# RMSNorm and QKV projection: DMA transposes from tile 6, stores in three parts, three staging buffers for wide weight chunks

## The chip, the cores and the metric

One core of one Trainium2 chip. The metric is the device time of one execution in microseconds (us). Engines: PE is the TensorE, PEld its weight loads, DVE the VectorE, ACT the ScalarE, POOL the GpSimd. SP is the SyncE, whose sequencer (SPq) issues nearly every DMA of this kernel, in program order.

## The reference

```python
def reference(x, gamma, w_qkv, eps):       # x: 8 x 1024 x 768, w_qkv: 768 x 2304, float32
    rms = np.sqrt(np.mean(x ** 2, axis=-1, keepdims=True) + eps)
    x_norm = x / rms * gamma
    return np.matmul(x_norm, w_qkv).astype(np.float32)
```

8192 rows make 64 tiles of 128 rows. A tile needs 6 blocks of K times 2304 columns of matmul, in bf16.

## The kernel before

x comes in as float32, is cast to bf16 and transposed, because the matmul needs K on the partitions. gamma goes into the weights, 1/rms into the evacuation of PSUM (the copy of a matmul's result out of the buffer in which the TensorE leaves it). The first six tiles (the head) are worked through while the six weight chunks arrive, chunk by chunk; the other 58 run tile by tile. Each operation is given a planned time, and all are issued in the order of those times.

```python
ARRIVALS = "wxxxwxxwxwww"                   # order of the head's loads
C0 = [0, 256, 2048, 512, 1024, 1536]        # columns at which the weight chunks begin
CHUNKS = [256, 256, 256, 512, 512, 512]
FIRST_XBAR = 12                             # first tile that a DMA transposes
...
PARTS = [(0, 1024), (1024, N - 1024)]       # a row of the output is stored in two parts
...
def load_w(c):
    n = CHUNKS[c]
    WF[c] = wst.tile([P, KO, n], f32, name=f"w_f{n}", bufs=3 if n == 256 else 2)
    nc.sync.dma_start(out=WF[c], in_=wv[:, :, C0[c]:C0[c] + n])
...
def trans_pe(t):                            # 6 transposing matmuls into PSUM, then copy_xT on DVE
    PT[t] = psum_t.tile([P, KO, P], bf16, name="pt")
    for ko in range(KO):
        nc.tensor.transpose(out=PT[t][:, ko, :], in_=XB[t][:, ko * P:(ko + 1) * P], identity=ident)
def trans_dma(t):
    XT[t] = xTp.tile([P, KO, P], bf16, name="xT")
    nc.sync.dma_start_transpose(out=XT[t], in_=XB[t])
...
for t in range(HEAD, MT):                   # HEAD is 6, MT is 64
    T = state["pe"]                         # planned start of the tile on PE
    at(T - 15, load_x, t)
    if t < FIRST_XBAR:
        at(T - 4.5, cast_x, t)
        at(T - 3.0, trans_pe, t)
        at(T - 2.5, copy_xT, t)
    else:
        at(T - 8.5, cast_x, t)
        at(T - 7.5, trans_dma, t)
    at(T - 5, stat, t)
    at(T - 3, recip, t)
    for n0, nl in n_tiles:                  # 4 blocks of 512 columns and one of 256
        unit(t, n0, nl)                     # matmuls, evacuation; store of a part when it is full
```

## Time and profile before

| | before |
|---|---|
| median of its runs | 394.45 us (393.62 to 394.56, 4 runs) |
| span of the profiled run | 392.1 us |
| PE busy | 98%, and 97% of the chain that ended last |
| transposing matmuls | 72, in 12 tiles |
| DMA packets' time, as a share of 16 engines' span | 97.1% |

The span is from the first to the last instruction; the time is some 2 us more. The chain that ended last is followed back from the last instruction, at each step to what released it. The lines that carry the argument (busy shares, the chain in order of time, three stretches) are shown and read in the prediction.

### The profile page before, as it was taken

The page shows a single profiled execution, that of the slowest core. Times are in us where ns is not written, and L with a number is a line of the kernel's source. Part 1 is how long each engine was busy: PE and PEld are TensorE (multiplying, and loading weights), DVE is VectorE, ACT ScalarE, POOL GpSimd, SP SyncE. Part 2 cuts the span into 40 slices and gives each one's busy share as a digit, 9 for nine tenths or more (in the row PEclk, how much of TensorE's full clock was granted, in tenths as well). Part 3 has the DMA queues.
Part 4 walks back from the last instruction along what each step waited for, and adds up shares of the span by engine and source line. Part 5 has one row for each costly group of instructions (what it writes and reads, how often), then busy time and mean ns, then how long its engine had stood idle before and what let it go on. Part 6 is the DMA issues. An engine that isn't in the chain of part 4 may idle for free.

```text
span 392.1 us, 5550 instructions
## 1 busy us (share of the span) xinstructions
PE 383.7 (98%) x2037; PEld 197.0 (50%) x2037; DVE 158.1 (40%) x319; ACT 182.8 (47%) x369; POOL 8.0 (2%) x18
## 2 busy tenths in 40 slices
PE   5999999999999999999999999999999999999996
PEld 2764455555455445545545545545545545545543
DVE  3853434443333433343434333434333443333332
ACT  5664344354444354345344445444444445444432
POOL 1221000000000000000000000000000000000000
PEclk9899999999999999999999999999999999999999
DMA  8989696899999999999999999999999999999974
GB/s 273 381 283 405 241 396 257 289 274 303 318 299 296 286 327 292 326 291 285 342 288 311 309 263 339 310 295 312 298 304 295 308 315 298 298 317 293 303 260 192
DMA packets 74423, 118.34 MB, mean 302 GB/s; under 512 B 44822, under 2 KB 47260, under 8 KB 74396
## 3 DMA queue, kind: packets, MB, share of 16 engines
q1 hardware_dynamic: 74384, 117.98, 97.1%
q8 instruction: 16, 0.26, 0.3%
q14 instruction: 11, 0.09, 0.1%
q10 hardware_dynamic: 12, 0.00, 0.0%
HBM read 32.25 MB, written 75.50 MB: 275 GB/s over the span
## 4 chain that ended last, share of the span: by engine, by line
PE 97%; DMA 1%; DVE 0%; ACT 0%; SPq 0%; issue 0%
PE pm L133 95%; DMA x_t<-in_x_dram 1%; PE pt L120 1%; DVE xb L102 0%; ACT ot L148 0%; DVE xT L124 0%; SPq L88 0%; ACT w_b L96 0%
## 5 line engine op out<-in xcount | busy, mean ns | idle before, releaser
L133 PE MATMUL pm<-w_b,xT 128*128 128x512 bf16 (+1 forms) x1956 | 376.4, 355 | 0.1
L133 PEld LDWEIGHTS <-xT 128*128 128x128 bf16 x1956 | 191.2, 98 | 181.4 <-issue 0.3
L146 DVE TENSOR_SCALAR ot<-pm,rstd 128x512 f32<-128x512 f32 (+1 forms) x163 | 112.2, 689 | 215.0 <-PE pm L133 200.5
L148 ACT ACTIVATE ot<-pm,rstd 128x512 f32<-128x512 f32 (+1 forms) x163 | 103.8, 637 | 199.6 <-PE pm L133 138.9
L107 ACT ACTIVATE sq<-x_t 128x768 bf16<-128x768 f32 x64 | 53.3, 832 | 0.0
L102 DVE CAST xb<-x_t 128x768 bf16<-128x768 f32 x64 | 35.1, 548 | 0.1
L109 ACT ACTIVATE rms<-ssq,eps_sb 128x1 f32<-128x1 f32 x64 | 18.9, 295 | 2.1
L107 ACT ACTIVATION_READ_ACCUMULATOR sq<-x_t 128x1 f32 x64 | 12.2, 191 | 0.0
L124 DVE COPY xT<-pt 128x768 bf16<-128x768 bf16 x12 | 6.7, 557 | 10.6 <-PE pt L120 10.3
L120 PE MATMUL pt<-ident,xb 128*128 128x128 bf16 x72 | 6.7, 235 | 3.6 <-DVE xb L102 3.5
L114 DVE RECIPROCAL rstd<-rms 128x1 f32<-128x1 f32 x64 | 9.8, 153 | 0.0
L96 ACT ACTIVATE w_b<-w_f,g_sb 128x256 bf16<-128x256 f32 (+1 forms) x12 | 6.7, 605 | 3.3 <-DMA w_f<-in_w_qkv_dram 3.3
L120 PEld LDWEIGHTS <-xb 128*128 128x128 bf16 x72 | 5.1, 104 | 6.1 <-DVE xb L102 4.7
L98 POOL TENSOR_SCALAR w_b<-w_f,g_sb 128x256 bf16<-128x256 f32 (+1 forms) x12 | 7.3, 623 | 23.9 <-DMA w_f<-in_w_qkv_dram 23.9
L94 DVE TENSOR_SCALAR w_b<-w_f,g_sb 128x256 bf16<-128x256 f32 (+1 forms) x12 | 4.9, 453 | 0.6 <-DMA w_f<-in_w_qkv_dram 0.6
L169 PE MATMUL pm<-warm 128*128 128x512 bf16 x8 | 3.6, 630 | 1.2 <-DVE warm L67 1.2
L169 PEld LDWEIGHTS <-warm 128*128 128x128 bf16 x8 | 1.0, 140 | 2.9 <-issue 1.7
L70 ACT ACT_TABLE_LOAD x1 | 1.3, 1283 | 1.3 <-PEq L247 1.3
L164 DVE COPY g_sb<-pt 128x6 f32<-128x6 f32 x1 | 0.2, 165 | 3.5 <-PE pt L163 3.5
L163 PEld LDWEIGHTS pt<-ident_f,g 6*128 6x128 f32 x1 | 0.2, 178 | 0.8 <-issue 0.8
L65 DVE MEMSET eps_sb<- 128x1 f32 x1 | 0.1, 59 | 0.8 <-PEq L247 0.8
L74 DVE CAST ident<-ident_f 128x128 bf16<-128x128 f32 x1 | 0.2, 226 | 0.2 <-POOL ident_f masks.py:199 0.2
(9 smaller groups left out, 1.6 us busy)
## 6 DMA issues: line engine op xcount, KB each, us to landing
out_dram<-ot SPq DMA_DIRECT2D x63, 640.0 KB, 3.9
out_dram<-ot SPq DMA_DIRECT2D x63, 512.0 KB, 3.9
x_t<-in_x_dram SPq DMA_DIRECT2D x64, 384.0 KB, 4.6
w_f<-in_w_qkv_dram SPq DMA_DIRECT2D x3, 1536.0 KB, 13.0
w_f<-in_w_qkv_dram SPq DMA_DIRECT2D x3, 768.0 KB, 6.4
out_dram<-ot SPq DMA_DIRECT2D x4, 256.0 KB, 2.0
xT<-xb SPq DMA_TRANSPOSE x52, 4.2
out_dram<-ot SPq DMA_DIRECT2D x1, 128.0 KB, 2.0
```

The lines of the kernel that those rows point to most:

```text
L94: nc.vector.tensor_scalar(out=o, in0=i, scalar1=g, scalar2=None, op0=mult)
L96: nc.scalar.activation(out=o, in_=i, func=AF.Copy, scale=g, bias=0.0)
L98: nc.gpsimd.tensor_scalar(out=o, in0=i, scalar1=g, scalar2=1.0, op0=mult, op1=mult)
L102: nc.vector.tensor_copy(out=XB[t], in_=X[t])
L107: nc.scalar.activation(out=sq, in_=X[t], func=AF.Square, accum_out=ssq)
L109: nc.scalar.activation(out=rms, in_=ssq, func=AF.Sqrt, scale=inv_k, bias=eps_sb)
L114: nc.vector.reciprocal(out=r, in_=RS[t])
L120: nc.tensor.transpose(out=PT[t][:, ko, :], in_=XB[t][:, ko * P:(ko + 1) * P], identity=ident)
L124: nc.vector.tensor_copy(out=XT[t], in_=PT[t])
L133: nc.tensor.matmul(out=PM[t, n0][:, :nl], lhsT=XT[t][:, ko, :], rhs=w_b[:, ko, n0:n0 + nl], start=(ko == 0), stop=(ko == KO - 1))
L146: nc.vector.tensor_scalar(out=o, in0=pm[:, :nl], scalar1=RS[t], scalar2=None, op0=mult)
L148: nc.scalar.activation(out=o, in_=pm[:, :nl], func=AF.Copy, scale=RS[t], bias=0.0)
```

## The change

Three edits. DMA transposes take tiles 6 to 11 off PE. Rows leave in three parts of 4096, 4096 and 1024 bytes. And all three wide weight chunks have a buffer at once, so that no load waits for one.

```diff
-FIRST_XBAR = 12
+FIRST_XBAR = 6
...
-    PARTS = [(0, 1024), (1024, N - 1024)]
+    PARTS = [(0, 1024), (1024, 1024), (2048, N - 2048)]
...
-        WF[c] = wst.tile([P, KO, n], f32, name=f"w_f{n}", bufs=3 if n == 256 else 2)
+        WF[c] = wst.tile([P, KO, n], f32, name=f"w_f{n}", bufs=3)
```

## The prediction

> **What bounds the kernel now.** I read the page first (busy shares, slices), then the chain that ended last in order of time, then stretches of the span, then the waits of the DMA queue. The busy shares name the TensorE, and the chain settles it, because a busy PE alone would not:
>
> ```profile
> PE 383.7 (98%) x2037; PEld 197.0 (50%) x2037; DVE 158.1 (40%) x319; ACT 182.8 (47%) x369; POOL 8.0 (2%) x18
> PE 97%; DMA 1%; DVE 0%; ACT 0%; SPq 0%; issue 0%
> L120 PE MATMUL pt<-ident,xb 128*128 128x128 bf16 x72 | 6.7, 235 | 3.6 <-DVE xb L102 3.5
> ```
>
> The chain is PE for 97% of the span, and nearly all of it is the main matmul (L133). L120 is the transposition of x on the PE: 12 tiles of 6. The chain in order of time shows what one such tile costs (start, length, what; all in us):
>
> ```profile
> 20.26 25.30 PE pm L133 x138
> 45.57 0.34 PE pt L120 x6
> 45.90 6.47 PE pm L133 x30
> 52.38 0.34 PE pt L120 x6
> 52.71 5.83 PE pm L133 x30
> 58.55 0.34 PE pt L120 x6
> ...
> 64.72 0.34 PE pt L120 x6
> 65.05 5.83 PE pm L133 x30
> 70.89 0.34 PE pt L120 x6
> 71.22 5.83 PE pm L133 x30
> 77.06 0.34 PE pt L120 x6
> 77.39 311.22 PE pm L133 x1602
> ```
>
> Three things are to be seen. From 20.26 on the PE waits for nothing. The six pieces of 0.34 between 45.57 and 77.06 are tiles 6 to 11, which come 6.17 apart, 5.83 of main matmuls and 0.34 of transposition. From 77.39 on, where DMA transposes feed the tiles, one piece of main matmuls runs to 388.61. (The 6.47 is no loss: the plan puts the transposes 3 us ahead of a tile, and the thirty matmuls between those two are five blocks of 512 columns, at 1.295 each, instead of four and a half.)
>
> The second resource is the DMA. Columns: length of the stretch; busy time and count of PE, PEld, DVE, ACT, POOL; PE clock; DMA share; GB/s.
>
> ```profile
> 52.00:60.00 8.00, 8.00 (x50) 4.29 (x49) 3.55 (x7) 3.18 (x6) 0.00 (x0) 1.00 1.02 389
> 60.00:77.00 17.00, 17.00 (x99) 8.99 (x98) 8.09 (x16) 7.73 (x16) 0.00 (x0) 1.00 0.71 253
> 100.00:340.00 240.00, 240.00 (x1235) 120.66 (x1234) 93.42 (x185) 111.77 (x226) 0.00 (x0) 1.00 1.03 304
> ```
>
> PE is full in each. The DMA share is 0.71 where the PE transposes and 1.03 where the DMA does, and yet the PE keeps 5.83 a tile. A share over 1 comes of packets that overlap, so 1.03 is not proof of a bound, only of little room.
>
> **What the Trainium skill says.** "TensorE: Matmul & The Clock Gate", section "Wait — 56ns, not 53.3ns?": warm matmuls follow each other at N/2.4 GHz plus about 2.5 ns, 55.6 ns for N = 128 and 215.7 for 512. The trace agrees: 24 x 215.7 + 6 x 109.2 (N = 256) = 5.83 us a tile, and 6 x 55.6 = 0.33 against the 0.34 in the chain. So the PE is at its issue rate, and the listed mean of 235 ns for a transposing matmul is latency, not cost. The same page, "Part 4: PE-mode transpose", gives about 275 ns in one kernel's context; that would make six cost 1.65, and the chain's 0.34 decides against using it as a cost here. "Advanced Engine Details and Errata", section "X-Bar Transpose (TRN2)", calls transposing DMAs as fast as ordinary ones. The trace differs: in 60:77 a tile takes 0.71 x 6.17 = 4.4 us of the DMA engines for 1.57 MB (0.39 in, 1.18 out), later 1.03 x 5.83 = 6.0; the 0.2 MB of a transpose thus add 1.6 us, where 0.55 would be in proportion (estimates, as packets overlap). "DMA: Bandwidth & Descriptors", section "Rules for kernel authors", advises coalescing small transfers; the third store part goes against it, and is priced below.
>
> **The change, part by part.**
>
> *DMA transposes from tile 6.* Removed from the PE: 6 tiles x 6 = 36 matmuls, all on the chain: 6 x 0.34 = 2.04 us. Removed from DVE: 6 copies from PSUM, 6 x 0.56 = 3.4 us, beside a PE that does not wait for DVE. Added: 6 DMA transposes, about 1.6 us of DMA each, in a stretch (45 to 77) that partly has room (0.71), and 6 issues on the DMA queue of about 1.6 us each. On the path: nothing, if they land in time. In the steady part the transpose for tile 12 was issued at 76.95, landed at 81.01, and the tile began at 85.2: 4 us of slack. For tile 6 there is less. It begins near 48.2 (48.5 before, less its own 0.34). The cast is planned 8.5 earlier, at 39.7, and x of tile 6 landed at 38.7 in the kernel before, so the issue is near 40.7. Stores in that stretch took 5.6 to 6.2 us to land against a median of 3.9, so I take 6: landed at 46.7, 1.5 us in hand. Tile 7: issue near 46, landing near 52, start near 54. Tile 8: issue near 52.3, landing near 58.3, start near 59.8.
>
> *Three store parts.* A row of 9216 bytes went as 4096 + 5120 and will go as 4096 + 4096 + 1024. In the trace's packet records the medians are 201 ns for 5120 bytes, 159 for 4096, 46 for 1024. So a tile has 8 packets more for each DMA engine and 8 x (159 + 46 - 201) = 32 ns more of its time, some 0.5% of 5.83. On the queue: one more issue a tile at 0.33, to 1.6 + 0.4 + 3 x 0.33 = 3.0 us of the 5.83. Part two leaves one block of 256 columns (0.65) earlier. In the head, six stores of the 256-column chunk can leave near 25 us instead of after 42, which makes the burst at 42 to 58 smaller (512 KB each instead of 640). In the tail nothing changes: the last tile is stored block by block in both.
>
> *Staging for all wide chunks.* The queue's longest wait goes:
>
> ```profile
> SPq L88 <- DVE w_b L94: 12.9, 1, 12.9
> ```
>
> The load of the last wide chunk was issued at 24.34 and landed at 31.06; it will be queued right behind the chunk that landed at 25.52 and arrive about 1 us sooner. Worth on the path: 0, because the chain has no wait from 20.26 on.
>
> Sum: -2.04 + 0 + 0. PE ends near 386.6, and the fixed end after it (392.1 - 388.6 = 3.5) stays: span 390.1. Time: 394.36 - 2.04 = 392.3.
>
> **The rivals.**
>
> *The early transposes come late.* The burst of head stores and its 1.02 share speak for it, the 1.5 us in hand, the smaller burst, and the six banks of PSUM (6.5 us of matmuls that need no evacuation) against it. If tiles 6, 7 and 8 each miss by 0.7 to 1, the gain is gone: 394.4, hardly over 395.
>
> *The DMA becomes the bound.* A share of 1.03 speaks for it. Against it: at the median packet times a tile needs 8 x (121 for a row of x, 3072 bytes, + 159 + 201) + 48 x 18 ns (256-byte transpose packets) = 4.7 us of each engine, 81% of 5.83, and the change adds 0.03. If I am wrong and the small packets cost 0.1 us on each of 52 tiles, 397.
>
> *The early chunk gains.* It would if the PE waited for weights; the chain shows no such wait after 20.26, and the earlier ones are for chunks whose issue does not change. If it did: 391.
>
> **Range and chances.** I take the first account, 392.3. The time before varies by 0.9 between its runs (393.62 to 394.54), which sets the width more than the mechanisms do; I stretch it upward for the first rival: 391.3 to 393.6. Over 2% faster would need under 386.5, with 5.8 us more than the change removes from the path: 0.01. Over 2% slower would need over 402.2, 0.19 us a tile lost from tile 6 on: 0.02. Within 2%: 0.97.
>
> **What would show it right or wrong.** Right: L120 falls to 36 matmuls; the last PE transposition in the chain is of tile 5, near 20; from there one piece of L133 to about 386.6 with tiles 5.83 apart; DMA share between 60 and 77 up from 0.71 to about 1. The queue has no wait of 12.9 on the last chunk, and the chunk lands near 30. Wrong: a wait of PE or its weight load on a DMA transpose between 45 and 62 (first rival); gaps that recur in the steady part, landings that grow beyond 4.2 (second); a different chain before 20.

## The result, and the profile after

| | before | after |
|---|---|---|
| median | 394.45 us | 392.41 us (392.06 to 392.93, 4 runs) |
| ratio | | 0.9954, 95% interval 0.9936 to 0.9972 |
| span of the profiled run | 392.1 us | 390.4 us |

A ratio is the mean time of one kernel's fast runs over that of the other's of the same rounds, so not quite the ratio of the medians. 392.3 had been predicted. The lines of the page that answer to those of before:

```profile
PE 380.2 (97%) x1964; PEld 195.6 (50%) x2001; DVE 154.4 (40%) x313; ACT 182.9 (47%) x369; POOL 8.1 (2%) x18
L133 PE MATMUL pm<-w_b,xT 128*128 128x512 bf16 (+1 forms) x1919 | 373.8, 355 | 2.1 <-ACT w_b L96 0.2
L120 PE MATMUL pt<-ident,xb 128*128 128x128 bf16 x36 | 4.0, 265 | 3.2 <-DVE xb L102 3.2
```

The transposing matmuls are halved, 72 to 36. One trap: L133 has 1919 matmuls here and 1956 before. Nothing was left out of the program; 37 records are missing from this trace (the weight loads are all 1956). Each missing one shows as a gap of some 0.05 us, which makes up most of the 2.1 us of idle time and cuts the chain, here in order of time (start, length, what), into many pieces:

```profile
16.80 3.27 PE pm L133 x30
20.41 5.88 PE pm L133 x48
26.34 10.74 PE pm L133 x49
37.13 10.74 PE pm L133 x49
...
379.65 7.10 PE pm L133 x38
386.77 0.47 ACT ot L148
```

No L120 piece stands between 20.41 and the end, where six stood before, and PE's last piece ends at 386.75, with 386.6 predicted. The stretches of the kernel after, with the columns as in the prediction:

```profile
52.00:60.00 8.00, 7.95 (x43) 4.19 (x43) 3.15 (x6) 3.18 (x6) 0.00 (x0) 1.00 1.06 361
60.00:77.00 17.00, 16.95 (x87) 8.42 (x87) 6.67 (x14) 7.88 (x17) 0.00 (x0) 1.00 1.05 341
100.00:340.00 240.00, 238.74 (x1214) 121.04 (x1237) 93.15 (x185) 112.36 (x226) 0.00 (x0) 1.00 1.03 305
```

From 60 to 77 the DMA share is 1.05 instead of 0.71: the transposes have moved there. The steady share of 1.03 is as before, three parts or two.

**A measure without the noise.** The times of one kernel differ by up to 1.7 us, which is near the size of the effect. The traces show where that comes from: the 151st main weight load, in the middle of the head, starts anywhere between 33.2 and 34.4 us in the fourteen traces. (In the two profiles of the changed kernel the spans differ by 0.74 us, and this start by 0.75.) From there to the last weight load, kernels that run the same PE program without a wait agree to 0.01 us. I call this the PE stretch. It is 354.68 before and 352.67 after: 2.01 us less, the 36 transposing matmuls at 56 ns.

### The profile page after: what moved, and what is told of

It reads as the page before. It is cut to its first block, busy times and chain, and to the rows that moved or that the text cites. A ratio compares the mean times of both kernels' runs of the same rounds, so it can differ in the third digit from the quotient of the medians.

```text
span 390.4 us, 5527 instructions
## 1 busy us (share of the span) xinstructions
PE 380.2 (97%) x1964; PEld 195.6 (50%) x2001; DVE 154.4 (40%) x313; ACT 182.9 (47%) x369; POOL 8.1 (2%) x18
## 4 chain that ended last, share of the span: by engine, by line
PE 96%; DMA 1%; issue 1%; DVE 0%; ACT 0%; SPq 0%
PE pm L133 95%; DMA x_t<-in_x_dram 1%; PE pt L120 1%; DVE xb L102 0%; ACT ot L148 0%; DVE xT L124 0%; SPq L88 0%; ACT w_b L96 0%
## 5 line engine op out<-in xcount | busy, mean ns | idle before, releaser
L133 PE MATMUL pm<-w_b,xT 128*128 128x512 bf16 (+1 forms) x1919 | 373.8, 355 | 2.1 <-ACT w_b L96 0.2
L133 PEld LDWEIGHTS <-xT 128*128 128x128 bf16 x1956 | 191.8, 98 | 182.9 <-issue 0.4
L120 PE MATMUL pt<-ident,xb 128*128 128x128 bf16 x36 | 4.0, 265 | 3.2 <-DVE xb L102 3.2
L120 PEld LDWEIGHTS <-xb 128*128 128x128 bf16 x36 | 2.8, 117 | 4.3 <-DVE xb L102 4.1
L124 DVE COPY xT<-pt 128x768 bf16<-128x768 bf16 x6 | 3.3, 556 | 2.6 <-PE pt L120 2.4
```

The source lines that it names most:

```text
L133: nc.tensor.matmul(out=PM[t, n0][:, :nl], lhsT=XT[t][:, ko, :], rhs=w_b[:, ko, n0:n0 + nl], start=(ko == 0), stop=(ko == KO - 1))
```

## The experiments

Each kernel gave a correct result.

### One part alone, and the change without its first part

`e1_transposes_only`: the kernel before, with `FIRST_XBAR = 6`.

> The kernel before with DMA transposes from tile 6 on, and nothing else of the change. Theory (the gain is 36 PE transposes off a PE-bound path, 0.34 us a tile): 392.3, 2.0 us below the kernel before, with 36 instead of 72 transposing matmuls. Rival (the stores and the staging make the room that the early transposes need, or bring part of the gain): clearly above 392.3, 393.5 or more, with a PE wait near tiles 6 to 9.

`e2_transposes_undone`: the changed kernel, with `FIRST_XBAR = 12`.

> The changed kernel with the first DMA transpose back at tile 12; three store parts and staging stay. Theory: the kernel before within 0.5 us, 394.4; the last chunk of weights still lands near 30 us, and that is worth nothing. Rival (staging or stores bring the gain): near 392.4.

`e5_parts_only`: the kernel before, with the three `PARTS`.

> The kernel before with three store parts alone. Theory: 394.4, within 0.5 us of the kernel before, although 63 more stores are issued and packets are smaller. Rival (the DMA is at its limit at a share of 1.03, so 32 ns a tile or more goes into the tile's period): 396 or more. Second rival (the parts help and hide a loss from staging): under 393.6.

`e6_staging_only`: the kernel before, with `bufs=3` for all chunks.

> The kernel before with a third buffer for wide weight chunks alone. Theory: the 12.9 us wait of the DMA queue goes, the last chunk lands about 1 us sooner, and the time stays 394.4 within 0.5 us. Rival (the head waits for weights in a way the chain hides): 393.6 or less.

Five rounds each, on one chip; the kernel before had a median of 394.15 there.

| kernel | median, us | ratio to before (95%) | PE stretch, us |
|---|---|---|---|
| transposes only | 393.37 | 0.9986 (0.9973 to 0.9999) | 353.56 |
| transposes undone (parts and staging) | 394.25 | 1.0006 (0.9990 to 1.0022) | 354.68 |
| parts only | 393.83 | 0.9998 (0.9981 to 1.0014) | 354.68 |
| staging only | 394.33 | 1.0004 (0.9990 to 1.0018) | 354.68 |

Parts and staging are worth nothing alone or together: the PE stretch is that of the kernel before to the hundredth. But the first run went against the theory. The transposes alone should have given 2.0 us and gave 0.8; the stretch shortens by 1.12 instead of 2.01. Its trace shows where 0.89 us went. Of the waits, those of the PE for a DMA (total, times, longest):

```profile
PEld L133 <- DMA xT<-xb: 1.0, 1, 1.0
PE pm L133 <- DMA xT<-xb: 0.7, 1, 0.7
```

One wait, seen twice: the weight load, and the matmul behind it, waited once for a transpose. (Tile 8's weight load was 0.12 us late too, too little for this list.) The chain of the same kernel between 58 and 69 us, in part, shows which:

```profile
58.60 1.36 PE pm L133 x8
59.96 6.82 DMA xT<-xb
66.78 0.05 issue
66.82 2.12 PE pm L133 x9
```

The fourth DMA transpose, that of tile 9, was issued at 59.96 and took 6.82 us to land (until the last of its parts was reported done), against a median of 4.2 for those whose landing the trace tells. Tile 9 could start only at 66.82. This is the first rival of the prediction (the early transposes come late), and here it is true, once. In the changed kernel the same transpose was issued at 58.20 and landed at 63.44, 2.1 us before its tile. So the lead is short there too, and something else in the change protects it. That became the new question.

### The size of the PE cost, and the room of the DMA

`e3_pe_until_36`: the changed kernel, with `FIRST_XBAR = 36`.

> The changed kernel with PE transposes up to tile 35: 30 tiles more than the changed kernel has. Theory (0.34 us of PE time a tile, no more and no less): 392.4 + 30 x 0.34 = 402.6. Rival (the DMA at a share of 1.03 sets a good part of the tile's period, so relieving it pays back): well under 402.6, 400 or less. Second rival (a PE transpose costs the 235 to 275 ns that a single one shows): 30 x 6 x 0.235 = 42 us more, 435.

Measured: 402.57 us (3 rounds), ratio 1.0201 (1.0184 to 1.0218). The PE stretch is 362.72, 10.05 more than in the changed kernel: 30 tiles x 0.335. The chain of this kernel, and two stretches of it, one with PE transposes and one with DMA transposes:

```profile
102.19 0.34 PE pt L120 x6
102.53 5.83 PE pm L133 x30
108.36 0.34 PE pt L120 x6
108.70 5.83 PE pm L133 x30
```

```profile
100.00:180.00 80.00, 80.00 (x469) 42.43 (x467) 36.13 (x72) 35.37 (x72) 0.00 (x0) 1.00 0.71 256
260.00:340.00 80.00, 80.00 (x414) 40.34 (x413) 30.53 (x60) 37.50 (x76) 0.00 (x0) 1.00 1.05 305
```

The DMA share falls from 1.05 to 0.71 where the PE transposes, and buys nothing: a tile's main matmuls take 5.83 in both. That settles that the DMA, with its share over 1, does not set the steady pace.

`e4_five_parts`: the changed kernel, with `PARTS` of 512, 512, 512, 512 and 256 columns.

> The changed kernel with rows stored in five parts, 4 of 2048 bytes and one of 1024. By the packet medians (85 ns for 2048 bytes against 159 for 4096) this adds 8 x (4 x 85 - 2 x 159) = 176 ns of each DMA engine's time a tile, and two issues of 0.33 us on the queue. Theory (4.7 of 5.83 us needed, hence room): 392.4 within 0.5. Rival (the DMA is the bound, or shares it): 58 x 0.18 = 10 us more, 402.

Measured: 392.53 us (3 rounds), ratio to the kernel before 0.9944 (0.9924 to 0.9964); the PE stretch is 352.67, as in the changed kernel. 126 more stores (tiles 0 to 62, two more each) with rows of 2048 bytes cost nothing. The transpose of tile 9 landed 3.9 us before its tile here; that of tile 6 had 1.5 us in hand, where it has 4.2 in the changed kernel. So this run only shifts which tile is tight, and none is late.

### How much lead a transpose needs

`e7_transposes_3us_later` and `e8_transposes_5us_later`: the changed kernel, with

```diff
-            at(T - 8.5, cast_x, t)
-            at(T - 7.5, trans_dma, t)
+            at(T - 5.5, cast_x, t)             # e8: T - 3.5
+            at(T - 4.5, trans_dma, t)          # e8: T - 2.5
```

> The changed kernel with cast and DMA transpose planned 3 us later (4.5 instead of 7.5 ahead of the tile). Theory (the transposes are hidden by about 4 us of lead, landing takes 4.3): the lead is nearly used up, issue near 5 us ahead: 392.4 to 395, with short PE waits in the crowded stretch of tiles 8 to 10 only. Rival (the lead does not matter, throughput does): 392.4 and no waits. Second rival (the lead was already short): above 400.

> As the last, with cast and transpose 5 us later than in the changed kernel (2.5 ahead). Theory: the transpose is issued about 2.7 us into the tile before and takes 4.3 to land, so a tile cannot start less than about 7.0 us after the one before: 58 x (7.0 - 5.83) = 68 us more, about 460, and the PE waits at each tile on the transpose. Rival (only throughput counts): 392.4.

| kernel | median, us | ratio to before (95%) | PE stretch, us | median issue, ahead of the tile |
|---|---|---|---|---|
| changed | 392.41 | 0.9954 (0.9936 to 0.9972) | 352.67 | 7.4 us |
| 3 us later | 395.77 | 1.0036 (1.0015 to 1.0057) | 355.93 | 4.9 us |
| 5 us later | 414.85 | 1.0514 (1.0493 to 1.0535) | 375.32 | 3.7 us |

3 us later lands a little above the expectation, and not where it said. The median lead left at landing is 0.4 us, so most tiles just make it, but four waits of note stand at 53.7, 165.8, 265.8 and 365.7; only the first is in the crowded stretch. The other three each begin 1 to 2 us after a packet of 16,384 bytes of the program's own instructions (at 164.2, 264.6 and 363.6), which takes a DMA engine for 0.9 to 1.2 us. Over the traces this is no accident. Take the transposes from tile 14 on whose landing can be told, in all traces but that of the next run: 125 had such a packet between issue and landing, with a median of 4.7 us, and 21 of them took over 5.4 us; 405 had none, with a median of 4.2, and the longest took 5.37. No run moved the packets, so the statistics show a link, not yet a cause.

5 us later, the work is unchanged and the time is 22 us longer: the transposes are on the path. In its list of waits:

```profile
PEld L133 <- DMA xT<-xb: 26.2, 32, 2.0
PE pm L133 <- DMA xT<-xb: 17.2, 25, 1.8
```

The kind of wait was as expected; its size and its number were not: 22.65 us more PE stretch, 0.39 a tile, where 68 us had been expected. Every tile was to lose 1.17; 32 of 58 waited, 0.8 us each. I had put the issue 3.1 us ahead of the tile and the landing at 4.3 us. Measured: 3.7 ahead in the median (to the tile's start as it was, waits included), and 3.7 to land. The DMA was emptier too (a share of 0.92 from 100 to 340 us, against 1.03); that this shortened the landings was not tested.

### What protects the early transposes

`e9_transposes_and_staging`, `e10_transposes_and_parts`: the changed kernel with one of the two other parts undone. `e11_transposes_only_2us_earlier`: the kernel before with

```diff
-FIRST_XBAR = 12
+FIRST_XBAR = 6
-        at(T - 15, load_x, t)
+        at(T - 17, load_x, t)
-            at(T - 8.5, cast_x, t)
-            at(T - 7.5, trans_dma, t)
+            at(T - 10.5, cast_x, t)
+            at(T - 9.5, trans_dma, t)
```

and `e12_changed_again`: the changed kernel.

> DMA transposes from tile 6 and staging, rows in two parts. New theory after the run with the transposes alone (393.4, with one PE wait of 0.84 us on the transpose of tile 9, which came 6.8 us after its issue in the crowd of head stores): what relieves the crowd is the store in three parts, which takes 0.79 MB out of the burst after 42 us; staging only moves one load by 1 to 2 us before 32. So this run keeps the wait near tile 9: 393.4. Rival (staging is what makes the room): 392.4 and no wait.

> DMA transposes from tile 6 and three store parts, two buffers for wide chunks. New theory (the parts make the room): 392.4 to 392.8, no PE wait on a transpose. Rival (staging makes the room): 393.4, with a wait near tile 8 or 9. Third possibility (both are needed): in between.

> The transposes alone, with load, cast and DMA transpose planned 2 us earlier (17, 10.5 and 9.5 ahead of a tile instead of 15, 8.5 and 7.5). New theory (the transposes alone fell short only by lateness of one or two of them): 2 us more lead cover the 0.84 of wait, 392.4 without parts or staging. Rival (the crowd of stores costs throughput, which lead does not buy): 393.4 or more.

> The changed kernel once more, on the same chip and beside the same runs of the kernel before as the three others: 0.995 of the kernel before, 392.4.

Five rounds, on one chip; the kernel before had a median of 394.42 there. For the first row the time is that of the earlier job; a dash says that the landing is not to be told from the trace.

| kernel | median, us | ratio to before (95%) | PE stretch, us | tile 8, tile 9: landed ahead of the tile, us |
|---|---|---|---|---|
| transposes only | 393.37 | 0.9986 (0.9973 to 0.9999) | 353.56 | -, 0.04 (waited) |
| and staging | 393.39 | 0.9975 (0.9962 to 0.9988) | 353.40 | -, 0.04 (waited) |
| and parts | 393.67 | 0.9981 (0.9966 to 0.9997) | 353.87 | 0.04 (waited), 0.04 (waited) |
| all three | 392.90 | 0.9959 (0.9946 to 0.9971) | 352.67 | 1.6, 1.8 |
| transposes only, 2 us earlier | 392.68 | 0.9951 (0.9938 to 0.9963) | 352.67 | 2.5, 2.7 |

The times alone would not settle it: the intervals of neighbouring rows overlap. The PE stretch does: 0.89, 0.73 and 1.20 us lost with the transposes alone, with staging, and with parts; nothing lost with all three, in both of its profiles. The weight loads' waits for a transpose, with staging and then with parts:

```profile
PEld L133 <- DMA xT<-xb: 0.8, 1, 0.8
PEld L133 <- DMA xT<-xb: 1.4, 2, 1.2
```

(With parts, the matmul's own wait at 66.78 is put down to the ScalarE, which ended at 66.75. The weight load, which waits for the transpose alone, started at 66.78 too, just after the landing at 66.74, so it was the transpose.)

The new theory, that the parts alone make the room, is wrong. The parts without staging are the worst of the three, by one trace each. Both are needed, and the DMA queue shows why. The first issues between 20 and 36 us, first with transposes and parts, then in the changed kernel:

```profile
24.44 0.37 SPq L88 DMA_DIRECT2D w_f<-in_w_qkv_dram  x1
24.85 9.57 SPq L152 DMA_DIRECT2D out_dram<-ot  x11
34.47 1.06 SPq L83 DMA_DIRECT2D x_t<-in_x_dram  x1
```

```profile
20.62 12.04 SPq L152 DMA_DIRECT2D out_dram<-ot  x11
32.71 1.21 SPq L83 DMA_DIRECT2D x_t<-in_x_dram  x1
```

Third parts of the head's six tiles are ready from 20.6 us on, since their weight chunk is the third to arrive. But the queue works in order, and ahead of those stores stands the load of the last wide chunk. With two buffers it waits until 24.44, and the queue's list of waits in that run has the line

```profile
SPq L88 <- DVE w_b L94: 12.9, 1, 12.9
```

as the kernel before has. The six small stores then go out behind it, land near 32 to 34 us and push everything else back: x of tile 6 is issued at 34.47 instead of 32.71, and its transpose 5.4 us ahead of the tile instead of 7.4. With a third buffer the load is issued at 11.28, five of the six small stores leave before 24 and the last at 25.53. (That 0.79 MB, 6 x 131 KB, are gone from the burst after 42 holds for both runs, so it does not tell them apart.) Staging without the parts frees the queue when there is nothing to issue: in that run the queue's long wait only changes its name, 12.1 us for the first full part to store.

The last row shows the other way out. With 2 us more lead and nothing else, the transposes alone give the whole 2.01 us. So the crowd costs lead, not throughput. No version is clearly faster than the changed kernel: 0.9951 and 0.9959 are not apart, and the PE stretch of both is 352.67.

**What made tile 9 late.** The packet records of the kept traces tell. A transpose is 768 packets of 256 bytes, 48 for each of 16 engines, so 720 are as many as fifteen engines have. In all five profiles a 16,384-byte instruction packet came near the end of tile 9's transpose (all in us):

| kernel | issue; ahead of the tile without a wait | packet 720 ended | instruction packet | last packet ended | landed |
|---|---|---|---|---|---|
| transposes only | 59.96; 6.0 | 64.59 | 64.45 to 65.62 | 65.87 | 66.78 |
| and staging | 59.91; 6.1 | 64.57 | 64.18 to 65.28 | 66.05 | 66.68 |
| and parts | 60.09; 5.6 | 64.56 | 64.48 to 65.50 | 65.94 | 66.74 |
| all three | 58.20; 7.3 | 62.58 | 62.62 to 63.80 | 62.86 | 63.44 |
| all three, again | 58.93; 7.4 | 63.71 | 63.72 to 64.85 | 63.95 | 64.51 |

("Without a wait" counts to 5.83 after the start of tile 8.) In the three runs that waited, no packet of the transpose moved for 0.80, 0.50 and 0.72 us, up to the end of the instruction packet (within 0.02 us); the last 8, 29 and 15 came in the 0.3 to 0.8 us after it. The records do not name the engine, but this is what one engine that is held up would leave. In the changed kernel there is no such hole. From packet 720 to the last took 1.3 to 1.5 us there, and 0.2 to 0.3 here: some 1.0 to 1.2 us of delay (an estimate, the difference), about as much as the whole wait of tile 9's weight load (0.96, 0.82 and 1.21).

So by these records the loss at tile 9 took two things. With parts or staging missing, the transpose has 1.2 to 1.8 us less lead; then the instruction packet takes about 1.0 to 1.2 us of what is left. The 1.8 to 2.1 us in hand of the changed kernel would have covered that packet (by the same estimate). What the crowd costs by itself is small here: tile 8, with no such packet near, was 0.12, 0.10 and 0.18 us late in the three runs. No run moved the instruction packet, so the split rests on the records alone, and whether it misses the transpose in the changed kernel by luck stays open.

## Why the prediction was right

- **PE transposes: -2.04 us.** Right. 2.01 in the PE stretch, and the slope holds for 30 tiles more (10.05 us). That 235 ns of a single one is latency and not cost was decisive; at 235 ns, 30 tiles would have cost 42 us.
- **Fixed end of 3.5 us.** Right: 390.4 - 386.75 = 3.6.
- **Early transposes in time, with 1.5 to 2 us in hand.** Right for the changed kernel: tile 8 had 1.3 and tile 9 had 2.1. For tile 6, 1.5 was too cautious; its transpose landed 3.2 us after its issue, not 6, and had 4.2 in hand. The tightest is tile 8, not tile 6: its transpose was issued at 52.76, behind the last stores of the head, and took 5.6 us.
- **Three parts: 0, and a smaller burst.** Right that it costs nothing (parts only, five parts). The burst was named as a help against the first rival, and it is, but only with staging. (In its sums, 0.19 us a tile to reach 402.2 from tile 6 on should be 0.17: 9.9 us over 58 tiles.)
- **Staging: 0.** Right alone, incomplete in the sum. The step "worth on the path: 0, because the chain has no wait from 20.26 on" looked at the PE's chain of before. Parts and staging have no worth of their own there, but together they give the transposes the lead that keeps them in time: with one of them or both missing, 0.7 to 1.2 of the 2.0 us are lost, most of it with an instruction packet in the way, which the prediction did not have in view. The prediction added three terms as if they were independent; the sum came out right because the change has all three. In that it was lucky.
- **First rival (late transposes).** Did not happen in the changed kernel, and did as soon as one helper was missing. Its size was too high: one tile, or nearly so, lost about 1 us, not three tiles. The six banks of PSUM, named against it, did not help: a matmul whose xT has not landed waits, as tile 9 did at 66.8.
- **Second rival (the DMA bound).** Refuted: packets added (five parts) and taken away (PE until tile 36), the pace is 5.83.
- **Third rival (the early chunk).** Refuted: staging only, 354.68. The chunk landed at 29.74, with "near 30" predicted.

## What to carry to other kernels

When one engine sets the pace, count what leaves its chain at the chain's own rate, and then ask how much lead each new transfer has. A busy DMA that does not bound throughput can still make one transfer late, by starting it late or by a packet in front of its last ones; more lead cures both. When one transfer is late, look at when its last packets moved, not only at how crowded the stretch was. In a queue that issues in order, a load that waits for a buffer holds back every store behind it, so an earlier store is worth something only if nothing ahead of it waits: two edits with no effect alone can be needed together.

## What the Trainium skill lacked or had wrong

- "Advanced Engine Details and Errata", section "X-Bar Transpose (TRN2)", has transposing DMAs as fast as ordinary ones. Here they are dearer. A transpose of 128 x 768 bf16 is 768 packets of 256 bytes at a median of 18 ns, 14 bytes a nanosecond for each engine, against 26 for 4096-byte packets (159 ns). From 60 to 77 us, a tile takes 0.71 x 6.17 = 4.4 us of DMA share without a transpose and 1.05 x 5.83 = 6.1 with one.
- "TensorE: Matmul & The Clock Gate", section "Part 4: PE-mode transpose", gives about 275 ns in a kernel's context. As a cost in a stream of matmuls the runs show 56 ns (2.01 us for 36; 10.05 for 180), which is what the section "Wait — 56ns, not 53.3ns?" of the same page gives for back-to-back matmuls of 128 columns (55.6 ns).
- "Runtime: NRT & Kernel Launch", section "Instruction fetch mechanics", says that programs are refilled in blocks of 16 KiB. The traces agree (15 to 17 packets of 16,384 bytes, some 25 us apart), but that section calls the cost of crossing a block mostly hidden and names none for other transfers; here each took 0.9 to 2.0 us, and in three runs the last packets of a transpose moved only when one had ended, with the PE's weight load waiting 0.8 to 1.2 us.
- On the time that the issuing queue itself loses in a crowd, the pages that I read give no figure. In the run with the transposes alone, the issue of a DMA transpose took 1.3 us at 40.8, 3.2 at 54.0 and 1.5 in the median over the run; that of a load of x rose from 0.44 to 1.25.
